# A decoder block on one core: pair tiles for the up projection, three batches of down sums, and partial sums written back into PSUM

## The chip, the core and the metric

The kernel runs on one core of a Trainium2 chip. The core has a matrix engine (TensorE, PE in the profile; PEld is its weight load), a vector engine (VectorE, DVE), a scalar engine (ScalarE, ACT), GpSimd (POOL) and SyncE (SP), which here only issues transfers. PE writes to PSUM, eight banks of 128 x 512 float32; the other engines read and write PSUM and the on-chip memory SBUF. Transfers from the chip's memory (DMA) are issued by SP, by ScalarE or by POOL. The metric is the device time of one execution in microseconds, as the median of several runs. The profile is one execution, taken by the hardware profiler.

## What is computed

One decoder block over 256 tokens with 2048 features, in float32:

```python
mod = silu(c) @ w_ada + b_ada                       # 2048 -> 6 x 2048
sh1, sc1, g1, sh2, sc2, g2 = split(mod, 6)
h = rms_norm(x, norm1_g) * (1 + sc1) + sh1
q, k, v, gb, gc, xt = split(h @ w_in, 6)            # w_in: 2048 x 6144, six parts of 1024
attn = causal attention of 8 heads of 128, q and k normalised per head
conv = gb * causal_dwconv(gc * xt, conv_w, conv_b)  # 3 taps along the tokens
mixed = concat(rms_norm(attn), rms_norm(conv))
x = x + g1 * (mixed @ w_out)                        # w_out: 2048 x 2048
h2 = rms_norm(x, norm2_g) * (1 + sc2) + sh2
u = causal_dwconv(h2 @ w_ffn_up, ffn_conv_w, ffn_conv_b)   # 2048 x 11264, 3 taps
u_gate, u_up = split(u, 2)
out = x + g2 * ((silu(u_gate) * u_up) @ w_ffn_down) # 5632 x 2048
```

The sequence has one block of 256 tokens, so the block-sparse attention of the full model is plain causal attention here.

## The kernel before

**Matmuls in two parts.** Every weight tile (128 x 2048 float32, 1 MB, "raw") is split into a rounded part `hi` (ScalarE, L329, `split_hi`) and a remainder `lo` (VectorE, `split_lo`, which shows as L166, the line of a wrapper through which most VectorE instructions are issued). Activations are split likewise. A product is hi x hi, hi x lo and lo x hi, all accumulated in PSUM.

**Slots.** The work is a list of slots, one weight tile each. A slot has its load, its size and a function that issues its matmuls. The last loop of the kernel goes through the slots; weights are split two slots ahead (`la`). Everything else is a task put at a slot with `at(slot, function)`: eviction, attention steps, convolutions, norms. Inside a slot tasks are sorted by a class from the table `cls`; the lists `x_first` and `hi_late` say for each slot whether splits come before or behind its tasks and matmuls. Each engine then runs its instructions in the order in which they were issued. Transfers of weights are issued by SP in the order in which the slots need them, together with the ada tiles (w_ada, 96 tiles of 1 MB), six or seven tiles ahead.

**Ada.** An `Ada` object makes some columns of `mod`: `consume` takes one tile and multiplies it with silu(c), either on PE (L396) or by VectorE's multiply-adds (L387, L389); `evac` and `cols` bring the sums into columns by transposes (L453). The list `ada` says at which slots. The first two (`ada_init`, scale and shift of the first 256 features) are consumed before slot 0; the next ones at slots 0 to 2. `gate_rows` places the 16 tiles of the last gate, and `fill` puts some ada tiles next to the second norm.

**Start.** x is loaded and transposed (`xn_tr`), normalised from PSUM by VectorE (`xn_norm`), shift and scale are made, and slot 0 runs in `go_first` (L583) with its own splitting in two halves.

**In projection: slots 0 to 47.** `turns` lists which of the twelve column groups of 512 (q0, q1, k0, ...) are advanced by which part of the 16 blocks of 128 input features. A pair (q0 and q1) takes two blocks a slot, a single group four. Each group has two banks (128 tokens each). Uses of a group at most three slots apart (`near`) stay in PSUM; otherwise `evac_in` empties the banks at the end: by a ScalarE copy into `pacc` the first time (L531), by a VectorE addition after that.

**Attention, short convolution, out projection.** Heads and convolution run as tasks during the rest of the in projection and the out projection (16 slots). The second norm follows at `N_OUT`.

**Up projection.** One unit is a group of 256 gate and 256 up columns: four slots of 16 + 16 matmuls in four banks (L1057 with both token parts, 512 wide, and L1060, 256 wide; the first groups use L1042). `up_sum` empties the banks into `ub`: ScalarE copies one half (L838), VectorE adds the other. `up_conv` and `up_conv_b` convolve gate and up columns (L806, L817 on ScalarE, additions on VectorE), `up_silu` and `up_gate` follow.

**Down projection.** The groups 0 to 15 are multiplied in half-slots (`A`: three products, 9 matmuls; `B`: four, 12 matmuls; L994 to L998), which form sums of a seven-product scheme. They lie between the up slots as `places` says. The groups come in batches; within a batch each of the four sets (column half, A or B) is summed over its groups in PSUM, then evicted by ScalarE (`evac_sum`, L934) and sent by POOL to memory, where later batches are added (L938, L940). `join_load` and `join_sum` fetch and combine them. The last six groups are multiplied plainly at the end (slots `LAST0` on), and `evac_down` writes the output.

## Time and profile before

| | us |
|---|---|
| median of 3 runs | 1146.89 (1146.16 to 1148.3) |
| profiled execution | 1144.87 |
| its span, first to last instruction | 1143.1 |
| PE busy in the span | 1128.9 (6035 matmuls and as many weight loads) |
| VectorE busy | 1064.0 |
| ScalarE busy | 730.6 |
| POOL busy | 61.3 |
| moved by DMA | 363.66 MB, 318 GB/s in the mean |

Busy times are the union of an engine's instructions in the profile. Matmuls overlap, so PE can be busy without going at its best pace; the pace is read from how much time a row of equal matmuls takes. A row of the groups gives line, engine, operation, output and inputs, shapes and count, then busy time and the mean of one in ns, then the engine's idle time just before and what ended it. A row of the timeline gives start and length in us. In the chain of work that ended last, each piece follows the one that released it.

### The profile page before, as it was taken

How to read it: one execution, taken by the hardware profiler on the slowest of the kernel's cores; microseconds unless marked ns; L12 is line 12 of the kernel's file. 1: busy time of each engine (PE TensorE's matmuls, PEld its weight loads, DVE VectorE, ACT ScalarE, POOL GpSimd, SP SyncE). 2: the span in 40 equal slices, each digit the busy share in tenths (PEclk: the TensorE clock that was granted, in tenths of full speed). 3: DMA queues.
4: the chain of work that ended last, by engine and by line, in shares of the span. 5: the costliest groups of instructions: out<-in, count | busy, mean ns of one | idle time of the engine just before them, and what ended most of it. 6: DMA issues, size and time to landing. Idle time of an engine off the chain costs nothing.

```text
span 1143.1 us, 16244 instructions
## 1 busy us (share of the span) xinstructions
PE 1128.9 (99%) x6035; PEld 953.8 (83%) x6035; DVE 1064.0 (93%) x1163; ACT 730.6 (64%) x1090; POOL 61.3 (5%) x90
## 2 busy tenths in 40 slices
PE   6999999999999999999999999999999999999998
PEld 4777778888888889988888888888888888888887
DVE  4789989989999998889999999899999999999798
ACT  4644455576786555566687676777677768866731
POOL 1000000000000000000000000101011101111000
PEclk9999999999999999999999999999999999999999
DMA  9999998998898899987679887999899988999951
GB/s 362 407 413 399 412 370 300 415 381 306 331 395 315 288 317 356 330 278 243 215 244 370 308 292 245 315 361 297 312 275 339 318 315 265 350 318 298 366 224 74
DMA packets 198687, 363.66 MB, mean 318 GB/s; under 512 B 9408, under 2 KB 108180, under 8 KB 194000
## 3 DMA queue, kind: packets, MB, share of 16 engines
q1 hardware_dynamic: 189152, 343.44, 82.8%
q0 software_dynamic: 8160, 17.04, 6.8%
q10 hardware_dynamic: 1296, 2.16, 0.5%
q8 instruction: 47, 0.77, 0.2%
q14 instruction: 32, 0.26, 0.1%
HBM read 343.70 MB, written 18.89 MB: 317 GB/s over the span
## 4 chain that ended last, share of the span: by engine, by line
PE 93%; DVE 3%; DMA 2%; SPq 1%; ACT 1%; issue 0%; DVEq 0%; ACTq 0%
PE z L1057 25%; PE z L1060 13%; PE u L996 4%; PE u L998 4%; PE u L994 4%; PE z L1042 4%; DMA raw<-in_w_in_dram 2%; DVE lo L166 2%; PE mk L516 1%; PE mk L517 1%; PE mk L514 1%; PE mx L516 1%; PE mc L516 1%; PE mq L517 1%; PE mg L516 1%; PE mx L517 1%
## 5 line engine op out<-in xcount | busy, mean ns | idle before, releaser
L329 ACT ACTIVATE hi<-raw 128x2048 fp32r<-128x2048 f32 (+1 forms) x227 | 417.8, 1857 | 260.5 <-DMA raw<-in_w_in_dram 73.2
L166 DVE TENSOR_TENSOR lo<-raw,hi 128x2048 fp32r<-128x2048 f32 (+2 forms) x229 | 501.7, 2200 | 23.0 <-ACT hi L329 17.7
L1057 PE MATMUL z<-h,hi 128*128 128x512 f32 x1280 | 303.3, 390 | 0.2 <-DVE ub L166 0.2
L1057 PEld LDWEIGHTS z<-h,hi 128*128 128x128 f32 x1280 | 237.8, 188 | 49.5 <-ACT hi L329 0.8
L389 DVE SCALAR_TENSOR_TENSOR ada<-raw,csil,ada 128x512 f32<-128x512 f32 (+3 forms) x167 | 195.7, 1175 | 5.3 <-DMA raw<-in_w_ada_dram 1.8
L1060 PEld LDWEIGHTS z<-h,lo 128*128 128x128 f32 x1280 | 163.1, 191 | 5.6
L1060 PE MATMUL z<-h,lo 128*128 128x256 f32 x1280 | 165.0, 283 | 0.0
L996 PE MATMUL u<-hi,gh 128*128 128x512 f32 x224 | 88.1, 393 | 0.0
L998 PE MATMUL u<-hi,gl 128*128 128x512 f32 x224 | 87.7, 392 | 0.0
L994 PE MATMUL u<-lo,gh 128*128 128x512 f32 x224 | 61.4, 390 | 0.0
L806 ACT ACTIVATE uy<-ub,fc,fc 128x256 f32<-128x256 f32 x88 | 47.6, 596 | 12.8 <-DVE ub L166 12.7
L938 POOL DMA_DIRECT2D down_sums<-pu x42 | 36.6, 1287 | 304.1 <-ACT pu L934 304.1
L996 PEld LDWEIGHTS u<-hi,gh 128*128 128x128 f32 x224 | 42.2, 188 | 9.9 <-ACT pu L934 2.8
L994 PEld LDWEIGHTS u<-lo,gh 128*128 128x128 f32 x224 | 42.0, 188 | 9.1 <-DVE lo L166 0.3
L998 PEld LDWEIGHTS u<-hi,gl 128*128 128x128 f32 x224 | 42.2, 189 | 7.4
L817 ACT ACTIVATE tap<-ub,fc 128x256 f32<-128x256 f32 x96 | 41.7, 502 | 0.0
L166 DVE TENSOR_TENSOR ub<-z,ub 128x256 f32<-128x256 f32 x96 | 33.8, 413 | 6.8 <-ACT ub L838 6.8
L301 DVE TENSOR_TENSOR raw<-raw 128x1024 f32<-128x1024 f32 x32 | 39.0, 1218 | 0.9 <-DMA raw<-in_w_ffn_down_dram 0.9
L1042 PE MATMUL z<-h,hi 128*128 128x256 f32 x256 | 36.4, 284 | 0.2 <-ACT h L765 0.2
L838 ACT ACTIVATE ub<-z 128x256 f32<-128x256 f32 x96 | 28.6, 383 | 12.1 <-PE z L1057 12.1
L166 DVE TENSOR_TENSOR uy<-tap,uy 128x510 f32<-128x510 f32 (+1 forms) x48 | 32.8, 684 | 2.0 <-ACT tap L817 0.2
L166 DVE SCALAR_TENSOR_TENSOR uy<-ub,fc,uy 128x254 f32<-128x254 f32 (+1 forms) x80 | 33.6, 477 | 0.6
(460 smaller groups left out, 1764.7 us busy)
## 6 DMA issues: line engine op xcount, KB each, us to landing
raw<-in_w_ada_dram SPq DMA_DIRECT2D x96, 1024.0 KB, 7.5
raw<-in_w_ffn_up_dram SPq DMA_DIRECT2D x176, 512.0 KB, 6.1
raw<-in_w_in_dram SPq DMA_DIRECT2D x47, 1024.0 KB, 8.0
raw<-in_w_ffn_down_dram SPq DMA_DIRECT2D x44, 1024.0 KB, 9.3
raw<-in_w_out_dram SPq DMA_DIRECT2D x16, 1024.0 KB, 6.0
raw<-in_w_ffn_down_dram SPq DMA_DIRECT2D x32, 512.0 KB, 5.0
down_sums<-pu POOLq DMA_DIRECT2D x56, 256.0 KB, 8.3
raw<-in_w_ffn_down_dram SPq DMA_DIRECT2D x32, 256.0 KB, 5.4
```

The source lines that it names most:

```text
L166: f(*a, **k)
L329: act(hi[:, :n], t[:, :n], AF.Copy)
L389: W.scalar_tensor_tensor(out=self.acc, in0=t[:, j, :], scalar=csil[:, i:i + 1], in1=self.acc, op0=ALU.mult, op1=ALU.add)
L516: mm(o, a, hi[:, k, s], start=(first and k == 0), stop=False)
L806: act(y[:, s], b[:, s], AF.Identity, bias=bias[:, i + j:i + j + 1], scale=w[2][:, i + j:i + j + 1])
L817: act(z[:, s], b[:, s], AF.Copy, scale=w[2 - d][:, i + j:i + j + 1])
L994: mm(bank_of(key), a, lo[:, n], start=False, stop=j in ends)
L996: mm(bank_of(key), a, hi[:, n], start=key not in begun, stop=False)
L998: mm(bank_of(key), b, hi[:, n], start=False, stop=False)
L1042: mm(o, w[:, j, a], h2T[k + j][:, v * 256:v * 256 + 256], start=begins and j == 0 and w is hi and not v, stop=ends and j == 3 and v == 1)
L1057: mm(zp[grp][ft], hi[:, j, ft * P:(ft + 1) * P], h2T[k + j], start=begins and j == 0, stop=ends and j == 3 and not late)
L1060: mm(zp[grp][ft][:, :256], lo[:, j, ft * P:(ft + 1) * P], h2T[k + j][:, :256], start=False, stop=ends and j == 3 and late)
```

## The change

Parts of it, with the names of the code:

- **Start.** Small matmuls that compute nothing needed (`keep_busy`, 34 in all) are put between the first steps. The last shift tile is loaded as two halves and multiplied in two steps; two one-column matmuls with a selecting vector replace its transposes and reduction. Slot 0's weights come in four DMAs instead of two, and its split, h and remainder are divided otherwise between ScalarE and VectorE. `norm_at` moves seven of the eight normalisations: four behind the first h products, three behind slot 0's split.
- **Seeds.** Where a group is taken up again, ScalarE copies `pacc` back into its two banks one slot before (`seed_in`), the matmuls accumulate onto that, and ScalarE copies the result out. Groups begun at the slots in `unseeded` keep the VectorE addition. Transposes set their start flag once a bank (`tr128`).
- **Pair tiles.** An up unit is now 512 gate columns (even units) or 512 up columns (odd units) of two groups, loaded by one DMA. Convolution, silu and product of both groups follow the units. ScalarE takes a second tap for the gate half.
- **Three batches.** Groups 0 to 5, 6 to 10 and 11 to 15 instead of four times four.
- **Columns.** Five small tables are transposed into one bank and evicted at once (`ffn_cols`).
- **Order.** `turns` exchanges neighbours (k before the second c, the first single g before x, c before v1); `places`, `gate_rows`, `fill_at`, the lists of lags and classes, `join`, `spill`, `back`, `x_first` and `hi_late` have new values.

```diff
-  [[0, 1, 2, 3], [4, 5, 6, 7], [8, 9, 10, 11], [12, 13, 14, 15]], [[0, 'A'], [1, 'A'], [0, 'B'], [1, 'B']],
-  [[0, 0, 3, 3], [0, 0, 0, 2, 2, 3], [1, 3], [1, 3, 3], [3], [0, 0, 0, 1, 1, 2, 2, 2, 3, 3], [1, 3],
-   [2, 2, 3], [3], [0, 0, 1, 1, 1, 2, 2, 2, 2, 3, 3], [1], [1, 3], [0, 0, 1, 1, 2, 2, 3, 3, 3],
-   [0, 0, 2, 3, 3], [2, 2, 2, 3, 3, 3], [0, 0, 2, 3, 3]]
+  [[0, 1, 2, 3, 4, 5], [6, 7, 8, 9, 10], [11, 12, 13, 14, 15]], [[0, 'A'], [1, 'A'], [0, 'B'], [1, 'B']],
+  [[], [0, 1], [0, 0, 0, 1, 2, 2, 2, 2, 2, 3], [0, 1, 3], [1, 1, 3], [1, 2, 3], [0, 1, 2, 3],
+   [0, 1, 2, 2, 3, 3, 3], [0, 1], [0, 0, 1, 3, 3], [0, 2, 3, 3], [0, 2, 2, 2, 3], [1, 2, 2, 3, 3, 3], [1, 3],
+   [0, 1, 2, 3, 3], [0, 2, 3]]
-  'join': [[-5, 1], [-2, 6]],       'fill_at': [0, 14, 11],   'taps': [1, 1, 2, 6],
+  'join': [[-6, 0], [0, 4]],        'fill_at': [-2, 16, 10],  'taps': [1, 2, 2, 6],
-  'spill': [6, 9],  'back': [-2, 0, -1, 1],  'up': [[0, 2, 2, 4], [0, 0, 0, 0]],
+  'spill': [9, 12], 'back': [-7, 2, -3, 5],  'up': [[0, 1, 2, 6], [0, 2, 1, 4], [0, 1, 1, 3], [0, 0, 0, 0]],
+  'busy': [9, 4, 5, 5, 5, 6],  'seed_lead': 1,  'norm_at': [1, 5, 8],
+  'unseeded': [0, 1, 2, 3, 4, 5, 6, 7, 8, 9, 10, 11, 12, 14, 15, 18, 19, 23, 39, 40, 41],
...
         if first:
-            mainp[key] = [bank(f"m{key}{t}") for t in range(3 if halves else 2)]
+            on_seed[key] = key in seeded
+            if key in seeded:
+                seeded.remove(key)
+                first = False
+            else:
+                mainp[key] = [bank(f"m{key}{t}") for t in range(3 if halves else 2)]
...
                 act(pacc[f, t], p, AF.Copy)
+            elif now[0] - 1 in unseeded.get(f, ()):
+                V.tensor_tensor(out=pacc[f, t], in0=p, in1=pacc[f, t], op=ALU.add)
             else:
-                V.tensor_tensor(out=pacc[f, t], in0=p, in1=pacc[f, t], op=ALU.add)
+                act(pacc[f, t], p, AF.Copy)
+    def seed_in(f):
+        mainp[f] = [bank(f"m{f}{t}") for t in range(2)]
+        for t in range(2):
+            act(mainp[f][t], pacc[f, t], AF.Copy)
+        seeded.add(f)
...
+            if i != uses[f][0] and not near(f, -1):
+                begun[f] = i
+                if i not in CFG["unseeded"]:
+                    at(len(slots) - 1 - CFG["seed_lead"], seed_in, f)
...
-            slots.append((w_load(w_up, k, 4, [(grp * 256, 256), (DFF + grp * 256, 256)]), 4, go))
+            slots.append((w_load(w_up, k, 4, [(grp % 2 * DFF + grp // 2 * 512, 512)]), 4, go))
...
+            w = grp % 2
+            for n, (f, *a) in zip(lag, ((up_conv, 0, w), (up_conv, 1, w), (up_gate if w else up_silu, 0), (up_gate if w else up_silu, 1))):
+                at(UP_SLOTS[-1] + 1 + hold + n, f, grp - w + a[0], *a[1:])
...
+    def keep_busy(b, n):
+        for _ in range(n):
+            mm(b[:, 256:384], onesr, onesr, start=True, stop=True)
...
+    keep_busy(p_one, w2)
+    sh.products(0, 0, 8)
     xn_tr(6, 7)
+    keep_busy(p_one, w3)
+    xn_norm(*range(5, n1))
+    sh.products(1, 0, 4)
+    sh.products(1, 4, 8)
+    keep_busy(p_one, w4)
+    rows_sum = t2k("adae")[:, :256]
+    act(rows_sum, sh.acc, AF.Copy)
+    for k in range(2):
+        mm(p_one[:, k:k + 1], rows_sum[:, k * P:(k + 1) * P], sel, start=k == 0, stop=k == 1)
+    keep_busy(bank("two"), w5)
+    z = small(8, "adaz")[:, :2]
+    V.tensor_copy(z, p_one[:, :2])
...
+    rest(0)
+    V.tensor_copy(hi[:, 1], w[:, 1])
+    rest(1)
+    act(hi[:, 2], w[:, 2], AF.Copy)
+    V.tensor_copy(hi[:, 3], w[:, 3])
+    xn_norm(*range(n1, n2))
+    for j in range(0, 4, 2):
+        V.tensor_tensor(out=lo[:, j:j + 2], in0=w[:, j:j + 2], in1=hi[:, j:j + 2].bitcast(F32), op=ALU.subtract)
```

More of the change, by code (lines that the diff above doesn't have):

```diff
@@ L226, in tile_block, with tr128 @@
     V.tensor_copy(identb, ident)
+    ssq = const.tile([P, 32], F32, name="ssq")
+    sel = ssq[:, :1]
+    V.tensor_reduce(out=sel, in_=ident.rearrange("p (j r) -> p j r", j=4)[:, :, 0], axis=AX.X, op=ALU.add)
     rows(vb, [(by_p(norm1_g[0]), 16)], nc.gpsimd)
+    def tr128(o, v, first):
+        nc.tensor.matmul(o, lhsT=v, rhs=ident, start=first, stop=True, is_transpose=True, skip_group_check=True)
     def to_cols(v, n, name):
@@ L362, in issue, with products @@
             def issue(t):
-                nc.sync.dma_start(self.view(t), w_ada[0, k0 * P:(k0 + self.rows) * P, a:a + self.n]
-                                  .rearrange("(k p) f -> p k f", p=P))
-            return issue
+                for i, j in self.cuts.get(r, [(0, self.rows)]):
+                    nc.sync.dma_start(self.view(t)[:, i:j], w_ada[0, (k0 + i) * P:(k0 + j) * P, a:a + self.n]
+                                      .rearrange("(k p) f -> p k f", p=P))
+            return issue
+        def products(self, r, i, j):
+            if i == 0:
+                self.used += 1
+                self.held = self.view(take((self, r)))
+            if self.acc is None:
+                self.acc = bank(f"ada{self.part}_{self.c0}")[:, :self.n]
+            for k in range(i, j):
+                q = 32 * (k % 4)
+                mm(self.acc[q:q + 32, :], crep[:, self.rows * r + k, :], self.held[:, k, :],
+                   start=r == 0 and k < 4, stop=r == self.tiles - 1 and k >= self.rows - 4,
+                   tile_position=(0, q))
+            if j == self.rows:
+                load_next()
         def home(self):
@@ L923, in gate_down @@
         done.add(f"gd{f}")
+        if f in CFG["sum_late"]:
+            return
         for t in range(2):
@@ L1498, in tile_block @@
     ada_init[0].consume(0)
+    def keep_busy(b, n):
+        for _ in range(n):
+            mm(b[:, 256:384], onesr, onesr, start=True, stop=True)
+    p_one = bank("one")
+    w0, w1, w2, w3, w4, w5 = CFG["busy"]
+    keep_busy(p_one, w0)
     pr = bank("n1b")
@@ L1511, in xn_norm @@
                             in1=rT.unsqueeze(1).to_broadcast([P, 2, 256]), op=ALU.mult)
-    xn_norm(0, 1, 2, 3)
-    ada_init[0].consume(1)
-    ada_init[0].evac()
-    ada_init[0].cols()
-    xn_norm(4)
+    sc, sh = ada_init
+    n0, n1, n2 = CFG["norm_at"]
+    xn_norm(*range(n0))
+    sc.consume(1)
+    keep_busy(p_one, w1)
+    sc.evac()
+    sc.cols()
+    hf = []
+    b1 = SH1 * NK
+    for k in range(2):
+        hf.append(t1k("hf"))
+        V.tensor_scalar(hf[k], xnT[0][:, k * 256:(k + 1) * 256], A1[:, k:k + 1], bcol[:, b1 + k:b1 + k + 1],
+                        op0=ALU.mult, op1=ALU.add)
@@ L1527, in tile_block @@
+    keep_busy(bank("two"), w5)
+    z = small(8, "adaz")[:, :2]
+    V.tensor_copy(z, p_one[:, :2])
     w = take(("w", 0))
     hi, lo = (sb.tile([P, 4, 512], F32R, tag=g, bufs=N_HL, name=g) for g in ("hi", "lo"))
-    parts = [(slice(2 * k, 2 * k + 2), t1k("hf"), t2k(f"h{k}", F32R)) for k in range(2)]
-    b1 = SH1 * NK
-    for k, (s, h, hk) in enumerate(parts):
-        hT[k] = halves(hk)
-        V.tensor_scalar(h, xnT[0][:, k * 256:(k + 1) * 256], A1[:, k:k + 1], bcol[:, b1 + k:b1 + k + 1],
-                        op0=ALU.mult, op1=ALU.add)
@@ L1548, in tile_block, with rest @@
-    for s, _, _ in parts:
-        V.tensor_tensor(out=lo[:, s], in0=w[:, s], in1=hi[:, s].bitcast(F32), op=ALU.subtract)
+    done.update((SH1, k) for k in range(2))
+    hk = [t2k(f"h{k}", F32R) for k in range(2)]
+    act(hi[:, 0], w[:, 0], AF.Copy)
+    for k in range(2):
+        hT[k] = halves(hk[k])
+        if k:
+            act(hT[k][0], hf[k], AF.Identity, bias=z[:, k:k + 1])
+        else:
+            V.tensor_scalar(hT[k][0], hf[k], z[:, k:k + 1], None, op0=ALU.add)
+    def rest(k):
+        V.scalar_tensor_tensor(out=hT[k][1], in0=hf[k], scalar=z[:, k:k + 1], in1=hT[k][0].bitcast(F32),
+                               op0=ALU.add, op1=ALU.subtract)
```

210 lines of the change are left out of this document (107 added, 103 removed), and 12 rows, old and new, of the table CFG.

## The prediction

> **What bounds the kernel now.** I read the page's busy times first, then busy time by stretch, PE's waits, and the chain of work that ended last in order of time.
>
> ```profile
> span 1143.1 us, 16244 instructions
> PE 1128.9 (99%) x6035; PEld 953.8 (83%) x6035; DVE 1064.0 (93%) x1163; ACT 730.6 (64%) x1090; POOL 61.3 (5%) x90
> ```
>
> ```profile
> core 0: us, PE busy (x) PEld busy (x) DVE busy (x) ACT busy (x) POOL busy (x), PEclk, DMA share, GB/s
> 0.00:22.00 22.00, 12.74 (x106) 8.48 (x106) 9.47 (x27) 9.79 (x15) 5.24 (x16) 1.00 0.95 348
> 22.00:26.00 4.00, 3.58 (x9) 2.86 (x10) 1.37 (x3) 1.82 (x3) 0.00 (x0) 0.57 1.02 420
> 26.00:42.00 16.00, 15.93 (x85) 12.13 (x87) 13.61 (x16) 9.65 (x11) 0.00 (x0) 1.00 1.07 397
> 170.00:320.00 150.00, 150.00 (x726) 123.85 (x725) 142.68 (x142) 97.86 (x219) 2.56 (x2) 1.00 0.91 344
> 870.00:970.00 100.00, 100.00 (x531) 86.09 (x530) 98.36 (x99) 73.13 (x94) 9.60 (x11) 1.00 0.95 305
> ```
>
> ```profile
> PE ada L396 <- DMA raw<-in_w_ada_dram: 1.2, 3, 0.5
> PE mx L516 <- ACT pa_g L531: 0.5, 1, 0.5
> PE z L1042 <- ACT h L765: 0.2, 1, 0.2
> PE z L1057 <- DVE ub L166: 0.2, 1, 0.2
> PE mq L517 <- DVE hl L166: 0.2, 1, 0.2
> ```
>
> ```profile
> 15.16 13.36 DMA raw<-in_w_in_dram
> ...
> 37.12 12.37 DMA raw<-in_w_in_dram
> ...
> 492.16 7.28 PE z L1057 x32
> 499.44 3.83 PE z L1060 x32
> ```
>
> The reader is to see four things. PE is busy 99% of the span, and the idle part lies before 22 us (12.74 of 22.00 busy); in the two later stretches shown it is never idle. A busy PE might still hide waits, so I look at its pace: the chain gives 7.28 us for 32 matmuls of 512 columns, 0.2275 us each, and 3.83/32 = 0.12 us for 256 columns. That pace holds through the chain, so PE runs at its issue rate. All waits of PE after 22.5 us that the list shows come to under 2 us. And up to about 50 us the chain runs over the weight DMAs (13.36 us, then 12.37 us), with a DMA share above 1 in the rows from 22 to 42 us. So a change can win at the start only if data lands sooner, later only those few waits; VectorE, at 93%, is a close second that nobody yet waits for.
>
> Here the row meets a rule that speaks for a gain. The Trainium skill ("Perfetto Trace Analysis", Identifying the Most-Contended Engine) says that matmul busy time misleads because matmuls overlap, and that the weight loads' busy share should be read instead. Here that is 83%, which by the rule would leave up to 17% to win. The constant 0.2275 us speaks against room of that kind.
>
> **The change, part by part.** The sum is made against the profiled execution, 1144.87 us: 1143.1 of span and 1.8 around it. The median of the runs shown, 1146.89, is 2.0 above; I add it at the end. Inside 0.2% (2.3 us) a run of this kernel can't be told from no change.
>
> *The start.* Rows of the first 42 us:
>
> ```profile
> 17.60 2.58 DVE L166 TENSOR_TENSOR xnT<-xn,n1rT 128x512 f32<-128x512 f32 x4
> 19.61 1.07 PE L396 MATMUL ada<-raw,crep 128*32 128x256 f32 x16 [0.54 <-DMA raw<-in_w_ada_dram]
> 20.74 0.38 ACT L417 ACTIVATE adae<-ada 128x256 f32<-128x256 f32 x1 [5.01 <-PE ada L396]
> 20.89 0.69 DVE L166 CAST hi<-raw 128x1024 fp32r<-128x1024 f32 x1
> 21.18 0.44 PE L453 MATMUL adac<-ident,adae 128*128 128x128 f32 x2 [0.50 <-ACT adae L417]
> 21.66 0.17 DVE L166 TENSOR_REDUCE adaz<-adac 128x2 f32<-128x8 f32 x1
> 21.86 0.51 ACT L1542 ACTIVATE h<-hf,adaz 128x256 fp32r<-128x256 f32 x1 [0.73 <-DVE adaz L166]
> 22.42 5.43 PE L583 MATMUL mc<-hi,h 128*128 128x512 f32 x16 [0.80 <-ACT h L1542]
> 23.62 1.06 ACT L1544 ACTIVATE hi<-raw 128x1024 fp32r<-128x1024 f32 x1 [1.26 <-DMA raw<-in_w_in_dram]
> 25.51 2.35 DVE L166 TENSOR_TENSOR lo<-raw,hi 128x1024 fp32r<-128x1024 f32 x2
> 29.50 0.39 PE L516 MATMUL mv<-hi,h 128*128 128x512 f32 x1
> 41.87 0.59 PEld L396 LDWEIGHTS ada<-raw,crep 128*32 128x32 f32 x16 [0.49 <-DMA raw<-in_w_ada_dram]
> ```
>
> The last shift tile now lands in two halves: only 8 of its 16 products are left when the second lands, so they end near 19.61 + 0.54 = 20.15. The ScalarE copy (0.38), two one-column matmuls for the two transposes (at most 0.44), one VectorE copy for the reduction (0.17) and the first h on VectorE (at most 0.51) follow: the first matmul near 21.5, 0.9 us sooner. The keep-busy matmuls, 34 of 128 columns at no more than 0.12 us each, go into idle PE time before that. But the second half of the weights lands at 23.62 as before. On VectorE the second cast (0.69/2) ends at 23.97; three normalisations are moved in behind it (3 x 2.58/4 = 1.94), so the two low parts (2.35) end at 28.26, and four matmuls later (0.9) the slot ends at 29.2 instead of 29.5: 0.3 us sooner.
>
> That lead meets the row at 41.87. There PE waits 0.49 us for an ada tile, executed in order behind slot 2. The change leaves the order of the loads up to there as it is, and the queue is full, so that tile lands at the same time, and a PE that comes earlier waits longer. I take 0 for the start; bounds: -2.7 (the 0.9, and 5.43 - 16 x 0.2275 = 1.8 of slow matmuls, if the tile lands sooner) and +0.5 (lead lost, low parts late). Single-bank column loads and one eviction for five are off the path: 0.
>
> *Seeding.* By the turns list, the code sums 54 tiles on VectorE now and 24 after; 14 weight groups (28 tiles) are instead written by ScalarE into PSUM one slot early, and copied out by ScalarE.
>
> ```profile
> L166 DVE TENSOR_TENSOR pa_g<-mg,pa_g 128x512 f32<-128x512 f32 x12 | 7.6, 681 | 0.0
> 30.43 2.04 ACT L531 ACTIVATE pa_c<-mc 128x512 f32<-128x512 f32 x4
> L881 ACT ACTIVATE gh<-uy 128x512 fp32r<-128x512 f32 x22 | 13.6, 633 | 6.5 <-DVE uy L166 6.5
> ```
>
> VectorE loses 30 x 0.68 = 20 us. ScalarE gains 28 copies out at 2.04/4 = 0.51, and 28 writes that the trace doesn't show: between 0.51 (reading PSUM) and 0.63 (SBUF to SBUF), I take 0.57 as the path lies between the two; 30 us together. They fall between slots 16 and 47, about 110 to 320 us, where ScalarE is busy 97.86 of 150 (170 to 320); two thirds of them there make it about 118 of 150. Cover: the split of weights runs two slots ahead, and a slot is 24 x 0.2275 = 5.5 us. A ScalarE command queued behind a seed (the next split, an attention step) is 1.1 us later. The seed waits for two free banks; the next slot's first matmul then waits for the seed, written a whole slot earlier. 0; bounds -0.2 and +1.5 (one late split at each of three crowded slots, 0.5 each).
>
> *Pair tiles, three batches.*
>
> ```profile
> raw<-in_w_ffn_up_dram SPq DMA_DIRECT2D x176, 512.0 KB, 6.1
> L934 ACT ACTIVATE pu<-u 128x512 f32<-128x512 f32 x56 | 28.7, 588 | 3.3 <-PE u L994 3.3
> L817 ACT ACTIVATE tap<-ub,fc 128x256 f32<-128x256 f32 x96 | 41.7, 502 | 0.0
> L166 DVE SCALAR_TENSOR_TENSOR uy<-ub,fc,uy 128x254 f32<-128x254 f32 (+1 forms) x80 | 33.6, 477 | 0.6
> L166 DVE TENSOR_TENSOR uy<-tap,uy 128x510 f32<-128x510 f32 (+1 forms) x48 | 32.8, 684 | 2.0 <-ACT tap L817 0.2
> 783.70 1.41 DVE L166 TENSOR_TENSOR ub<-z,ub 128x256 f32<-128x256 f32 x4
> ```
>
> The up weights come in 88 DMAs of 1 MB instead of 176 of 512 KB, the same bytes: SP issues less, PE never waited for them, 0. The matmuls stay the same in number and shape. Fourteen partial sums fewer go out: 14 x 0.588 = 8.2 us of ScalarE, 14 POOL transfers, all beside PE: 0. The first tap on ScalarE for 16 groups takes 2 x 0.477 - 0.684 = 0.27 us each off VectorE (4.3 us) and puts 2 x 0.502 each on ScalarE (16 us). ScalarE: 731 + 30 - 8 + 16 = 769 us, 67%; VectorE: 1064 - 20 - 4 = 1040, 91%.
>
> The half-slots move. Before, every unit of up matmuls but one ends with a down half-slot, under which its four banks are emptied. The one without it is at 783.70: ub's additions begin as the next unit is due, and PE waits 0.2 us, some 0.5 with its restart. After, two units end so with a batch open: +0.5. The wait at z L1042 (0.2) stays. Where VectorE was just in time, 24 us less work could spare me about as much: -0.5. Bounds of this part: -1.0 and +4.8 (below).
>
> *What only moves.* Two of the four fill products go ahead of the second norm instead of into it: the same PE work in the same gap, so the wait at z L1042 can move by its 0.2 either way. The 16 loads of the last gate change slots, each with a VectorE sum, in SP's queue between weight loads that are there over a slot ahead; the spill of x1 (ScalarE's queue) goes later, its return (SP's) up to five slots earlier or four later, ahead of its use. Other order lists say only whether a split goes before or after the work of its slot. I take 0, covered by the lead of the splits; without that cover, one split late costs its slot at most 0.5, which is in the bounds of the parts above.
>
> *The tail.* The last matmul, addition and store don't change. Sums for the down outputs are joined earlier or later by slots of 5.5 us, before the slots that need them. 0, bounds -0.2 and +0.5.
>
> Sum: 0 + 0 + 0.5 - 0.5 + 0 = 0. So 1144.9 against the profiled execution, 1146.9 in terms of the median.
>
> **The rivals.** *The start pays (faster).* The granted clock is 0.57 from 22 to 26 us, which is 0.43 x 4 / 0.5 = 3.4 us at half speed, and the first 16 matmuls took 5.43 us. If the keep-busy matmuls hold the clock, the chain to z is shorter and the tile at 41.87 lands sooner too, all 2.7 us come through: 1144.2. For it: the clock. Against: the DMA chain of 13.36 and 12.37 us, whose order is kept. Chance 0.14. The Trainium skill ("TensorE: Matmul & The Clock Gate", Part 1: The HAM clock gate) says that the clock halves after an idle window of about 3.4 us and returns after a busy one, which agrees with the 3.4 us worked out above; by it the 1.8 us would be won, if nothing behind them waits.
>
> *PE hides waits (faster).* If the weight loads' 83% is the true load, 24 us less on VectorE could show whole: 1123. The constant pace leaves 0.03.
>
> *Bursts of pairs (slower).* Gate and up columns of two groups now end together: convolutions, two products and two roundings fall behind one unit, 2.7 us of tap additions (4 x 0.684) and 1.4 of products in a row, where VectorE is at 98.36 of 100. The lows of the next half-slots queue behind. If the burst outlasts the lead by 0.3 to 0.6 us at each of eight pairs, PE loses 2.4 to 4.8: 1149.3 to 1151.7, 1150.5 in the middle. It decides from 0.3 us a pair. For it: 98.36. Against: 4.3 us less work there, and a lead of up to two slots. Chance 0.20.
>
> *The change doesn't do as it says.* Only 14 of 26 later groups are seeded, the rest stay on VectorE. As nobody waits for these additions the time is the same, 1146.9; it is part of the forecast.
>
> **How the numbers follow.** Forecast (no change that can be told) 0.60; start pays 0.14, hidden waits 0.03, and 0.03 for PE's other waits all going with a little of the start (1144.5): faster 0.20. Slower 0.20. Predicted is the likeliest, 1146.9. The range reaches from just under the start's 1144.2 to the middle of the slow case: 1144.0 to 1150.5, leaving out 0.03 below and about half of the 0.20 above. The forecast's own range is 1145.0 to 1149.0.
>
> **What would show it.** PE's first matmul into mc near 21.5 and clock 1.00 there, but the ada product at slot 2 still near 41.9 behind a longer DMA wait: the start as told. If it comes at 40 or earlier, the start's rival holds. VectorE near 1040 us and ScalarE near 770: the exchange as counted. Seeds of 0.51 to 0.63 us, none followed by a wait of PE. Waits of PE for ub at two units without a half-slot, 0.5 each; many waits for lo or ub between 570 and 1070 would make the prediction wrong upward, PE starting slots of the in projection over 1 us sooner after 60 us wrong downward.

## The result: 8.6 us slower, and the profile after

The changed kernel takes 1155.04 us in the median (1153.51 to 1157.06), the kernel before, run beside it, 1146.47 (1144.93 to 1148.3). The ratio is 1.0078, 95% interval 1.0066 to 1.0089. That is outside the predicted range (1144.0 to 1150.5). The profiled execution took 1153.51 us; its page begins:

```profile
span 1151.7 us, 16091 instructions
PE 1132.5 (98%) x6072; PEld 956.8 (83%) x6072; DVE 1046.5 (91%) x1120; ACT 762.2 (66%) x1160; POOL 49.4 (4%) x76
```

VectorE lost 17.5 us of work and ScalarE gained 31.6, close to what was counted (1040 and 769 us were forecast). PE did the same work but for 37 small matmuls more, 34 of them the keep-busy ones, and yet the span is 8.6 us longer. The head of the list of PE's waits after 22.5 us (total us, times, longest):

```profile
PE m('D', 3)2_10285 L550 <- DVE d L172: 1.4, 1, 1.4
PE n2b L791 <- DVE n2d L172: 1.2, 1, 1.2
PE z L1110 <- DVE ub L172: 1.0, 1, 1.0
PE m('D', 0)0_9944 L548 <- DVE lo L172: 0.9, 1, 0.9
PE mc L630 <- DVE lo L172: 0.6, 1, 0.6
PE ada L424 <- DMA raw<-in_w_ada_dram: 0.4, 1, 0.4
```

Five of these six name VectorE, the engine that was relieved. To see where the time went, I take the start of the same slot in both traces, with PE's work in between set equal where half-slots moved. PE is behind by 1.5 us at the first up matmul, 3.4 at the first matmul of the last stage, 6.8 after the last matmul, and 8.6 at the end of the span. The rows for the first three, of the timeline of PE, before and then after:

```profile
425.92 0.74 PE L1042 MATMUL z<-h,hi 128*128 128x256 f32 x4 [0.24 <-ACT h L765]
1073.74 0.40 PE L516 MATMUL m('D', 0)0_10003<-hi,gh 128*128 128x512 f32 x1
1139.11 0.64 PE L514 MATMUL m('D', 3)2_10339<-lo,gh 128*128 128x256 f32 x4
```

```profile
427.40 0.74 PE L1095 MATMUL z<-h,hi 128*128 128x256 f32 x4 [0.24 <-ACT h L818]
1077.18 0.50 PE L550 MATMUL m('D', 0)0_9944<-hi,gh 128*128 128x512 f32 x1
1145.86 0.64 PE L548 MATMUL m('D', 3)2_10285<-lo,gh 128*128 128x256 f32 x4
```

So there are three places: 1.5 us up to the second norm, 1.9 in the up stage, and 3.3 + 1.9 in the last stage (up to the last matmul, and behind it).

**The last stage.** The timeline of VectorE before and then after, where it first needs the last gate (`ju<-ju,ada`, `gate_down`):

```profile
1089.73 4.48 DVE L166 TENSOR_TENSOR lo<-raw,hi 128x2048 fp32r<-128x2048 f32 x2
1094.13 0.68 DVE L166 TENSOR_TENSOR ju<-ju,ada 128x512 f32<-128x512 f32 x1
```

```profile
1089.50 6.78 DVE L172 TENSOR_TENSOR lo<-raw,hi 128x2048 fp32r<-128x2048 f32 x3
1102.46 0.69 DVE L172 TENSOR_TENSOR ju<-ju,ada 128x512 f32<-128x512 f32 x1 [6.18 <-DMA ada<-gate_sums]
```

VectorE stands still for 6.18 us, until the broadcast of the gate lands. Before, it had no such wait, and it had no room for one either: it was busy 9.93 of 10 us from 1090 to 1100.

```profile
1090.00:1100.00 10.00, 10.00 (x46) 8.28 (x45) 9.93 (x9) 4.01 (x5) 0.00 (x0) 1.00 1.05 407
```

(PE, weight loads, VectorE, ScalarE, POOL, clock, DMA share, GB/s; 10 us of before.) After the gap VectorE works without a pause to 1147.9; PE waits for its low parts and for a bank (0.9 and 1.4 us above), and the end of the additions after the last matmul comes another 1.9 us later. Why the gate is late stands on POOL's queue, before and then after:

```profile
1052.63 3.49 POOL L938 DMA_DIRECT2D down_sums<-pu  x4 [29.72 <-ACT pu L934]
1069.08 1.97 POOL L433 DMA_DIRECT2D gate_sums<-adar  x4 [12.97 <-ACT adar L431]
1076.36 0.56 POOL L439 DMA_DIRECT2D ada<-gate_sums  x1 [5.31 <-DMA gate_sums<-adar]
```

```profile
1080.56 3.49 POOL L991 DMA_DIRECT2D down_sums<-pu  x4 [41.15 <-ACT pu L987]
1082.72 3.28 POOL L461 DMA_DIRECT2D gate_sums<-adar  x4
1094.58 0.56 POOL L467 DMA_DIRECT2D ada<-gate_sums  x1 [8.58 <-DVE lo L172]
```

The last four partial sums, which are added in memory, left 16 us ahead of the gate's four small writes; now they leave straight ahead of them. The writes land 10.2 us after their issue instead of 5.1 (median of the four), straight behind the last of the partial sums (1093.3, then 1093.5 to 1094.0), and the broadcast goes out only then. (The row names a VectorE release; but in every profile where no partial sums are issued between the writes and the broadcast, it goes out 0.6 to 0.7 us after the last write landed, here at 1093.96.) The Trainium skill ("DMA: Bandwidth & Descriptors", SWDGE vs HWDGE vs iDMA) says that only one queue is allocated to transfers issued by GpSimd; the doubled time behind 1 MB of accumulating transfers agrees with that.

**The second norm.** In front of the sums for the norm VectorE now adds the last scale tile, moved from slot 55 to 58. Before, then after:

```profile
418.19 0.15 DVE L166 TENSOR_REDUCE ss<-ss 128x2 f32<-128x6 f32 x1
```

```profile
416.61 3.11 DVE L417 SCALAR_TENSOR_TENSOR ada<-raw,csil,ada 128x512 f32<-128x512 f32 x4
419.63 0.15 DVE L172 TENSOR_REDUCE ss<-ss 128x2 f32<-128x6 f32 x1
```

That explains a part of the 1.5 us. 0.9 of it arises behind the fourth column block of the out projection, with the wait for `n2d`, and does so again in other profiles with the same order. The rest was there before and is not fixed: three profiles whose kernels are the same up to this point (changed kernel, gate back, half-slots early) come to that block 0.6 and 1.2 us behind the kernel before, and 0.5 ahead of it.

**The up stage.** PE loses 1.1 us at 656 (0.95 of it a wait), behind a run of half-slots. Rows of VectorE, ScalarE and PE, then 20 us of the windows (after, then before):

```profile
652.01 1.23 DVE L313 TENSOR_TENSOR raw<-raw 128x1024 f32<-128x1024 f32 x1 [2.10 <-DMA raw<-in_w_ffn_down_dram]
654.86 1.92 ACT L341 ACTIVATE hi<-raw 128x2048 fp32r<-128x2048 f32 x1 [4.25 <-DVE raw L319]
657.56 0.73 PE L1110 MATMUL z<-h,hi 128*128 128x512 f32 x2 [0.95 <-DVE ub L172]
```

```profile
640.00:650.00 10.00, 10.00 (x46) 8.28 (x45) 8.50 (x5) 6.99 (x5) 0.00 (x0) 1.00 1.04 404
650.00:660.00 10.00, 9.04 (x48) 7.48 (x47) 7.73 (x10) 5.75 (x11) 0.00 (x0) 1.00 1.04 405
```

```profile
640.00:650.00 10.00, 10.00 (x53) 8.56 (x52) 9.83 (x10) 5.07 (x4) 0.00 (x0) 1.00 0.79 265
650.00:660.00 10.00, 10.00 (x53) 8.60 (x52) 9.93 (x11) 7.96 (x14) 2.07 (x4) 1.00 1.02 368
```

The weights land late with the DMA engines full (share 1.04, 404 GB/s, where before had 0.79); VectorE's weight sums wait for them, ScalarE's next split for VectorE, the copies into `ub` queue behind that split, and PE waits for `ub`.

### The profile page after: what moved, and what is told of

Read it like the earlier page. It is cut to its first block, busy times and chain, and to the rows that moved or that the text cites. A ratio compares the mean times of both kernels' runs of the same rounds, so it can differ in the third digit from the quotient of the medians.

```text
span 1151.7 us, 16091 instructions
## 1 busy us (share of the span) xinstructions
PE 1132.5 (98%) x6072; PEld 956.8 (83%) x6072; DVE 1046.5 (91%) x1120; ACT 762.2 (66%) x1160; POOL 49.4 (4%) x76
## 4 chain that ended last, share of the span: by engine, by line
PE 85%; DVE 7%; DMA 5%; issue 1%; ACT 1%; SPq 0%; DVEq 0%; ACTq 0%
PE z L1110 23%; PE z L1113 12%; PE z L1095 4%; PE u L1047 4%; PE u L1051 4%; PE u L1049 4%; DVE lo L172 3%; DMA raw<-in_w_in_dram 2%; DMA raw<-in_w_ffn_down_dram 2%; PE mk L550 1%; PE mk L551 1%; PE mk L548 1%; PE mx L550 1%; PE mc L550 1%; PE mq L551 1%; PE mg L550 1%
## 5 line engine op out<-in xcount | busy, mean ns | idle before, releaser
L1110 PEld LDWEIGHTS z<-h,hi 128*128 128x128 f32 x1280 | 238.2, 188 | 50.4 <-DVE ub L172 1.9
L870 ACT ACTIVATE tap<-ub,fc 128x256 f32<-128x256 f32 x128 | 54.5, 506 | 0.0
L859 ACT ACTIVATE uy<-ub,fc 128x256 f32<-128x256 f32 x88 | 48.0, 601 | 8.8 <-DVE ub L172 8.6
L172 DVE TENSOR_TENSOR uy<-tap,uy 128x510 f32<-128x510 f32 x64 | 43.9, 685 | 3.5 <-ACT tap L870 0.2
L991 POOL DMA_DIRECT2D down_sums<-pu x28 | 24.4, 1287 | 283.4 <-ACT pu L987 283.4
L1095 PEld LDWEIGHTS z<-h,hi 128*128 128x128 f32 x256 | 33.2, 192 | 0.5 <-ACT h L818 0.5
```

The lines of the kernel that those rows point to most:

```text
L172: f(*a, **k)
L859: act(y[:, s], b[:, s], AF.Identity, bias=bias[:, i + j:i + j + 1], scale=w[2][:, i + j:i + j + 1])
L870: act(z[:, s], b[:, s], AF.Copy, scale=w[2 - d][:, i + j:i + j + 1])
L1095: mm(o, w[:, j, a], h2T[k + j][:, v * 256:v * 256 + 256], start=begins and j == 0 and w is hi and not v, stop=ends and j == 3 and v == 1)
L1110: mm(zp[grp][ft], hi[:, j, ft * P:(ft + 1) * P], h2T[k + j], start=begins and j == 0, stop=ends and j == 3 and not late)
```

## The experiments

One table first, since the same three places are read in every trace: PE's lag behind the kernel before at the first up matmul, its growth from there to the last stage, and its growth within the last stage up to the last matmul. These come from one profile each; the column "that run" is the time of that execution, which can lie some us off the median. "Of it clock" is the part of the two growths in which the granted clock was below 1.00 (time at half clock, halved).

| kernel | at first up matmul | + up stage | + last stage | of it clock | that run | median us | ratio to before |
|---|---|---|---|---|---|---|---|
| changed kernel | 1.5 | 1.9 | 3.3 | 0 | 1153.51 | 1155.04 | 1.0078 |
| gate back | 0.4 | 3.2 | 0.0 | 0 | 1148.93 | 1151.17 | 1.0043 |
| before, gate late | -0.2 | 1.2 | 0.1 | 0 | 1145.96 | 1145.79 | 0.9998 |
| no seeds | 1.5 | 7.6 | 3.8 | 3.4 | 1159.69 | 1156.16 | 1.0092 |
| no keep-busy | 0.7 | 3.2 | 4.8 | 0 | 1155.43 | 1153.18 | 1.0068 |
| scale tile back | 2.8 | 5.7 | 0.0 | 0 | 1153.87 | 1153.56 | 1.0059 |
| half-slots spread | 2.7 | 4.2 | 0.0 | 0 | 1152.00 | 1153.65 | 1.0060 |
| half-slots early | 2.1 | 10.6 | 0.1 | 3.4 | 1157.86 | 1157.24 | 1.0089 |
| before, half-slots and gate late | -0.3 | 2.0 | 9.6 | 1.7 | 1156.12 | 1156.11 | 1.0083 |
| loads back | 0.2 | 12.5 | 4.0 | 1.7 | 1163.51 | 1164.20 | 1.0150 |
| loads and gate back | 0.1 | 12.4 | 0.0 | 1.7 | 1157.56 | 1159.19 | 1.0114 |
| loads in light units | 0.0 | 13.9 | 0.0 | 3.4 | 1159.01 | 1159.96 | 1.0121 |
| pairs, four batches | 0.1 | 14.5 | 0.7 | 3.4 | 1160.39 | 1161.84 | 1.0135 |
| the same, old order | 1.6 | 15.2 | 0.7 | 3.4 | 1162.51 | 1162.03 | 1.0137 |
| before, three batches | 2.0 | 9.9 | 5.3 | 3.4 | 1164.23 | 1162.98 | 1.0143 |
| gate's sums first | 1.0 | 3.5 | 0.1 | 0 | 1150.01 | 1149.88 | 1.0038 |
| memset moved | 1.4 | 7.9 | 0.0 | 3.4 | 1154.61 | 1152.84 | 1.0051 |

So a wait of PE can cost more than itself. In the trace of "no seeds" PE waits 3.19 us, and the 12 matmuls behind the wait take 5.49 us, 0.46 each instead of 0.2275; the granted clock (third figure from the end of the second row) is 0.50 there:

```profile
659.85 5.49 PE L1110 MATMUL z<-h,hi 128*128 128x512 f32 x12 [3.19 <-DVE ub L172]
660.00:665.00 5.00, 5.00 (x12) 3.94 (x13) 4.97 (x7) 5.00 (x12) 0.99 (x2) 0.50 0.99 351
```

Each such stretch lasts about 3.4 or 6.8 us and so costs 1.7 or 3.4. It does not follow every wait: one of 2.7 us at the same place in "no keep-busy" left the clock at 1.00. The changed kernel's own trace has none.

### The gate back

```diff
-'slag': [[2, 2], [0, 3]],
+'slag': [[2, 2], [-1, 2]],
```

> The changed kernel with one pair of numbers set back: the sums of the last gate are taken one slot before the tail and spread at slot 2 of it (slag of G2 -1, 2 instead of 0, 3). Theory (the gate's broadcast holds VectorE 6.2 us in the tail, and VectorE has no idle time after that): the wait for gate_sums goes, PE reaches its last matmul about 3.3 us sooner and the end after the last matmul shrinks from 5.2 to 3.3 us; about 5 us less than the changed kernel, 1150 us. Rival (the tail is long because its sums and evictions were reordered, joins at 0 and 4, evac_down in the last class): at most 1 us less, 1154 us.

Measured 1151.17 (1148.93 to 1151.76), 3.9 us less than the changed kernel; the wait for the gate is gone, and the last stage adds nothing up to the last matmul (0.6 us stays behind it). The theory held for the place; some 4 of the 5 us that it forecast came off.

### The gate late in the kernel before

```diff
-'slag': [[1, 2], [-1, 2]],
+'slag': [[1, 2], [0, 3]],
```

> The kernel before with only the last gate's sums and spread put later (slag of G2 0, 3 instead of -1, 2). Theory (gate broadcast alone makes the tail long): VectorE waits about 5 us for gate_sums around slot 3 of the tail and the time rises by 3 to 5 us over before, 1150 to 1152 us. Rival (it takes the other moves of the change as well): within 1 us of before.

Measured 1145.79 (1144.41 to 1148.77), ratio 0.9998 (0.9988 to 1.0007). My theory fell: the broadcast lands at 1092.6, still ahead of VectorE, which is due at the gate at 1094.6. So the later slot by itself costs nothing, and "the gate is late" is not yet the cause.

### No seeds

```diff
+'unseeded': list(range(48)),
```

> The changed kernel without any seed: all later sums of the in projection are VectorE additions again, all else as changed. Theory (seeds are off PE's path): the time stays within 1 us of the changed kernel, 1154 to 1156 us; VectorE 20 us busier and ScalarE 30 us less busy. Rival (the seeds cost part of the 8.6 us, by bank waits or a crowded ScalarE): 2 us or more less than the changed kernel.

Measured 1156.16 (1153.76 to 1159.69), though VectorE was busy 1062.2 us again and ScalarE 736.5. Seeding neither wins nor loses anything that can be told.

### No keep-busy matmuls

```diff
-'busy': [9, 4, 5, 5, 5, 6],
+'busy': [0, 0, 0, 0, 0, 0],
```

> The changed kernel without the 34 keep-busy matmuls. Theory (PE waits at about 42 us for an ada tile whose landing is fixed by the transfers): the granted clock falls to half for about 3.4 us near slot 0 again, slot 0 takes up to 1.5 us longer, but slot 4 starts within 0.5 us of the changed kernel (50.0 us) and the total stays within 1 us of it. Rival (keep-busy matmuls win time that is kept): 1.5 us or more slower than the changed kernel; or, if they delay the first steps, about 0.5 us faster.

```profile
22.00:26.00 4.00, 4.00 (x11) 3.13 (x12) 3.67 (x8) 0.78 (x2) 0.00 (x0) 0.60 1.03 421
```

The clock in the first slot is 0.60 in this profile and 1.00 in the changed kernel's. That the small matmuls make the difference is not shown: of the four profiles of kernels with the old start, which has none of them, the kernel before shows 0.57, but the three others (gate late, half-slots and gate late, three batches) show 1.00. The row of "gate late":

```profile
22.00:26.00 4.00, 3.57 (x14) 2.46 (x15) 1.99 (x3) 2.38 (x4) 0.00 (x0) 1.00 1.02 418
```

There slot 0 ends at 28.37 us instead of 29.50 before, and of these 1.1 us 0.2 are left at the first up matmul. So the clock at the start wins little that lasts, and the time without the small matmuls is not longer: 1153.18 (1152.82 to 1155.43), ratio 1.0068 (1.0053 to 1.0083), an interval that overlaps the changed kernel's. PE's first matmul into mc comes at 21.96 us without them, against 22.3 to 23.2 in nearly all profiles with them, so they may hold up the first steps by some 0.5 us.

### The scale tile back, with the gate back

```diff
-[3, 8, 512, False, 58, 7]
+[3, 8, 512, False, 55, 7]
```

> The changed kernel with the last gate's sums and broadcast again one slot before the last stage (as in the run that put them back alone, 1151.2), and with the tile of the second norm's scale, columns 8 to 15, loaded from slot 55 again instead of 58. Theory: the 3.1 us of that tile's VectorE additions at 416.6 stand ahead of the second norm's sums and delay the first up matmul by about 1.4 us, so this one ends at 1149.9 (1149.4 to 1150.3), PE's wait n2b <- n2d of 1.2 us is gone, and the first up matmul starts within 0.5 us of where it starts before. Rival: the lag at the norm comes from the attention and the output projection ahead of it (other classes), and the additions are hidden: 1151.2, the wait stays.

Measured 1153.56 (1151.38 to 1154.37), 2.4 above the run with the gate back: a miss. The additions no longer stand ahead of the norm, but in the out projection, where VectorE has almost no gap either (9.76 of 10 us from 380 to 390), and PE waits 1.5 us for a low part up to 389. At the norm the wait stayed, for another reason:

```profile
424.91 1.80 POOL L399 MEMSET ada<- 128x2048 f32 x1 [91.11 <-DVE n2r L172]
424.94 1.92 DVE L172 TENSOR_SCALAR n2d<-ident,n2r 128x128 f32<-128x128 f32 x2
```

Two scalings that take 0.48 us in the kernel before took 1.92 beside GpSimd's filling of the gate's sum tile. The changed kernel loads that gate from up slot 4 on instead of 11, which brings the filling to the norm.

### Half-slots spread

```diff
-[[], [0, 1], [0, 0, 0, 1, 2, 2, 2, 2, 2, 3], ... [0, 1],
+[[1, 3], [0, 1, 3], [0, 1, 1, 2, 2, 2, 3], ... [0, 3],
```

> The run with the scale tile at slot 55, and four half-slots of the down projection moved within the list: two into the first unit, one into the second, so that the run of six in the third unit's place 2 is shorter, and one moved in the ninth unit so that it ends with a half-slot. Theory: the stall of 1.1 to 1.6 us at 656 us comes from a unit that ends without a half-slot after a run of them, during which the splits of the weights are late; spread out, both units' stalls (1.1 to 1.6 at 656, 0.2 at 748) go and this one ends 1.3 to 1.8 us under the run with the scale tile alone, about 1148.3. Rival: the stall follows from the pairs themselves (additions into ub late behind the partner's convolution) and stays or moves to another unit: no difference.

This is on top of the run before. Measured 1153.65 (1152.0 to 1153.88), no difference from it: the stall came one unit earlier (the lag grows from 2.8 to 4.4 us between 620 and 640). The rival, "moves to another unit", held.

### Half-slots early, gate late

```diff
-[0, 1, 2, 3, 3], [0, 2, 3]]
+[0, 1, 2, 3, 3], [0, 0, 0]]
```

> The changed kernel with its late gate kept as it is (sums at the first slot of the last stage, broadcast at its fourth), but the last three half-slots of the down projection put right after the first up slot of the last unit instead of after its first, third and fourth, so that the last four partial sums leave ScalarE some 8 us sooner. Theory: the late gate costs only because those four copies (2.0 us) stand ahead of the gate's copy on ScalarE and their four accumulating transfers ahead of the gate's on GpSimd's queue, whose small writes then take 10 us to land instead of 5 to 6; with them gone VectorE's wait of 6.2 us falls under 1 us and the time to 1150.5 to 1152. Rival: it is the later slot by itself, in a kernel whose last stage starts 3.4 us late, and the time stays within 1 us of 1155.

The mechanism held, the time missed: the small writes land after 4.5 us, VectorE's wait is gone and the last stage adds 0.1. But the up stage adds 10.6 (three half-slots in a row bring two waits for low parts at 1058 and 1064, 3.7 us in sum; the stall at 659 is 2.5; half clock costs 3.4), and the time is 1157.24 (1155.5 to 1157.86).

### Half-slots and gate late in the kernel before

```diff
-[0, 0, 2, 3, 3], [2, 2, 2, 3, 3, 3], [0, 0, 2, 3, 3]]   'join': [[-5, 1], [-2, 6]],   'slag': [[1, 2], [-1, 2]],
+[0, 0, 2, 3, 3], [2], [0, 2, 3]]                       'join': [[-5, 1], [0, 6]],    'slag': [[1, 2], [0, 3]],
```

> The kernel before with the late gate (which alone made no difference) and, of the change, one more thing: the last four half-slots of the down projection at the end of the list (after slots 1, 3 and 4 of the last unit and one before), so that their partial sums leave as the last stage begins, and the loads that join them two slots later. Theory: now the gate's broadcast lands after VectorE is due at it; VectorE waits 3 to 6 us near 1094 and the kernel takes 1149 to 1152. Rival: the kernel before has slack for it, 1146 to 1147.

Measured 1156.11 (1153.7 to 1157.76), ratio 1.0083: more than forecast. On POOL and on VectorE it is the pattern of the changed kernel:

```profile
1078.77 3.49 POOL L938 DMA_DIRECT2D down_sums<-pu  x4 [55.17 <-ACT pu L934]
1081.76 2.46 POOL L433 DMA_DIRECT2D gate_sums<-adar  x4
1094.89 0.56 POOL L439 DMA_DIRECT2D ada<-gate_sums  x1 [10.68 <-DVE ju L166]
```

```profile
DVE ju L166 <- DMA ada<-gate_sums: 6.3, 1, 6.3
```

The late gate that cost nothing alone now holds VectorE for 6.3 us, once the last partial sums stand ahead of it. Of the 9.6 us of the last stage 6.5 are waits of PE and 1.7 half clock. (The run also joins the second half's sums two slots later, whose share is not separated.)

### The gate's loads back; with the gate back; in light units

```diff
-'gate_rows': [3, 10, 18, 22, 30, 32, 33, 45, 49, 53, 54, 57, 59, 68, 72, 75],
+'gate_rows': [10, 14, 17, 18, 30, 35, 40, 43, 46, 51, 54, 57, 58, 64, 68, 74],   # loads back; loads and gate back
+'gate_rows': [10, 14, 18, 22, 24, 26, 28, 30, 38, 40, 42, 44, 46, 48, 58, 66],   # in light units, gate back
```

> The changed kernel with one list put back: the slots at which the 16 tiles (1 MB each) of the last gate are loaded are those of the kernel before. Theory: the stalls of PE near 656 us (1.1 us in the changed kernel's trace, 1.6 to 4.4 in the traces of its variants) and near 860 us (0.4 to 3) come from three gate tiles loaded in the 30 us before a run of ten half-slots, and four in the 60 us before a run of seven; the DMA engines are full there and the weights land late. With the loads apart, PE's lag behind the kernel before grows by less than 0.5 us between 620 and 690, and the time falls by 1 to 3 us, to 1152 to 1154. The tail's wait for the gate stays. Rival: the runs of half-slots alone fill the DMA engines and VectorE; the stall stays above 1 us and the time within 1 us of 1155.

> The changed kernel with the last gate's loads at the slots of the kernel before, and its sums and broadcast at theirs (which alone gave 1151.2). Theory: the two causes add; the tail costs nothing, the stalls of the up stage are gone, and what stays is the 1.3 us at the second norm and the end: 1148 to 1149.5. Rival: the stall at the runs of half-slots stays: 1151 to 1152.

> As the run with both put back, but the last gate's 16 loads stand at slots of units that hold few half-slots or none (five of them from the first two units on, none beside the runs of seven and ten). Theory: the loads collide with the half-slots' weights, so this is no slower than the run before, 1147.5 to 1149, and the share of the DMA engines from 600 to 640 us is lower. Rival: the loads only move the crowding into the units where VectorE is busy already, and a wait of 1 us or more appears there: 1150 to 1152.

My theory fell: 1164.2 (1159.17 to 1164.92), 1159.19 (1155.84 to 1160.42) and 1159.96 (1159.01 to 1160.39). In the first of them PE waits at three units' ends (655, 720 and 753 us) instead of one, and at two of these VectorE has an addition of the last gate straight ahead of the additions into `ub` (at 655.38, shown, and at 719.73):

```profile
PE z L1110 <- DVE ub L172: 6.0, 3, 2.8
655.38 2.35 DVE L417 SCALAR_TENSOR_TENSOR ada<-raw,csil,ada 128x2048 f32<-128x2048 f32 x1
657.64 1.41 DVE L172 TENSOR_TENSOR ub<-z,ub 128x256 f32<-128x256 f32 x4
```

Each of the 16 loads brings VectorE 2.35 us and the DMA engines 1 MB, and both other lists that I tried were worse than the changed kernel's. So taking the loads away from the runs of half-slots does not lift the stalls; at two of these three waits it is the 2.35 us on VectorE that stand in the way. The gate back took 5.0 us off here as well (1164.2 to 1159.19).

### Pairs with four batches, also with the old order; three batches without pairs

The first has the changed code with the old `plan`, `gate_rows`, `join`, `slag`, `gate`, `back`, `spill` and the old classes of `join_sum` and `evac_down`; the second also the other old classes (but for `up_conv_b`), `x_first`, `hi_late`, `ada`, `qk`, `evac`, `sq` and `tr`; the third is the kernel before with the change's values of the first list.

> The changed kernel's code with pair tiles and seeding, but with the four batches of the kernel before, its places of the half-slots, its slots for the last gate's loads, sums and broadcast, and its steps of the tail (joins, gate, spill, and the order of the last sums and evictions). Theory (the placement costs, not the pairs): the tail's 3 to 5 us are gone as in the run with the gate put back, the stalls at the units' ends stay under 1 us in sum, and what is left is the 1 to 1.5 us at the second norm: 1147 to 1149. Rival (pairs cost: convolutions and products of two groups come in one burst, and the units' ends without a half-slot wait for VectorE's additions): waits of 3 us and more for ub or lo between 570 and 1070 us: 1150 to 1156.

> As the run with four batches, and nearly all other order numbers of the kernel before as well (which of a slot's tasks goes first, the splits' order lists, the scale tile at slot 55); of the change there stay the start, the seeding and the pair tiles with their own steps. Theory: the second norm's 1 to 1.5 us go too, 1145.5 to 1147, no difference from before that can be told. Rival (pairs cost): 1149 to 1155; the tasks' order was part of what made pairs possible, and it may be slower than the run with four batches.

> The kernel before, without pairs, seeding or the new start, with three batches and the changed kernel's places of half-slots, its slots for the last gate's loads, sums and broadcast, and its steps of the tail. Theory (the placement costs): VectorE waits 3 to 6 us for the gate near 1096 us, PE loses 3 to 5 us in the tail and 1 to 5 us at the runs of half-slots: 1150 to 1156. Rival (it is the pairs): 1146 to 1148.

All three are slower than the changed kernel, and than all that I had forecast for them: 1161.84 (1160.39 to 1162.56), 1162.03 (1161.12 to 1164.39) and 1162.98 (1162.09 to 1164.23). The first, pairs with the old places, has its largest wait (half clock follows it) where the old list puts half-slots behind the first slot of the first unit:

```profile
PE u L1049 <- DVE ub L172: 4.8, 1, 4.8
```

That place is empty in the change. The third, without pairs, seeds or the new start, has stalls at the changed kernel's unit ends (1.6 us at 658) and a wait for the gate of 8.2 us. So neither the pairs alone nor the placement alone is faster. That pairs need the half-slots later, and that these then bring the runs and the late partial sums, is my reading; each list was fitted to its own kernel, and no run separates that. These runs do part the 0.9 us at the second norm. With the gate's loads at their old slots, and so no memset at the norm, 0.5 is left (the first run, and the three runs with other load slots); with the scale tile back at 55 as well (the second, which comes to that block 1.6 us late) nothing is left.

### The gate's sums first

```diff
-'sum_rows': 1,
+'sum_rows': -2,
```

> The changed kernel with its late gate kept at its slots; of the first slot of the last stage's tasks, the gate's sums go first instead of last, so that on ScalarE the gate's copy stands ahead of the last four partial sums (2.0 us) and on GpSimd's queue the four small writes ahead of the four accumulating transfers of 256 KB. Theory: the small writes land after about 5 us instead of 10, the broadcast goes out 5 to 7 us sooner, VectorE's wait of 6.2 us near 1096 falls under 2 us, and the time to 1151 to 1153. Rival: the wait follows from the late slot, whatever stands ahead; it stays above 4 us and the time within 1 us of 1155.

```profile
1081.60 1.97 POOL L461 DMA_DIRECT2D gate_sums<-adar  x4 [41.26 <-ACT adar L459]
1083.57 3.56 POOL L991 DMA_DIRECT2D down_sums<-pu  x4
1088.05 0.56 POOL L467 DMA_DIRECT2D ada<-gate_sums  x1 [0.92 <-PE m('D', 1)1_9985 L551]
```

Measured 1149.88 (1148.96 to 1155.75), ratio 1.0038 (1.0023 to 1.0053): 5.2 us less than the changed kernel by the medians, 4.6 by the ratios, and a little more than forecast. (The class holds for both gates, so the first gate's sums, near 323 us, move within their slot as well; the lag at the first up matmul, 1.0 us, is within what the other profiles show.) The gate's writes start 1.1 us sooner, land after 4.3 us instead of 10.2, the broadcast goes out 6.5 us sooner, and VectorE has no wait for it. This isolates the cause in the last stage: not the slot but what stands ahead of the gate's sums in it. Of the 6.5 us, 1.1 come from the earlier start of the last of the four writes and 5.4 from its shorter landing.

### The memset moved

```diff
-'gate_rows': [3, 10, 18, ...     (with the scale tile and the gate back)
+'gate_rows': [6, 10, 18, ...
```

> As the run with the scale tile at slot 55 (1153.6), with the first of the last gate's loads at the seventh up slot instead of the fourth, and with it the filling of its sum tile by GpSimd (1.8 us), which in that run began 0.03 us before VectorE scaled the identity for the second norm: those two scalings then ended after 1.92 us instead of 0.48. Theory: VectorE waits for GpSimd there; the scalings take 0.48 us again, PE's wait for them (1.2 us) and its lag at the first up matmul (2.8 us) shrink by 1.2 to 1.4, and the time by 1 to 1.5 if nothing later absorbs it. Rival: the scalings are slow because of their place behind the out projection's evictions; they stay at 1.9 us.

```profile
424.87 0.48 DVE L172 TENSOR_SCALAR n2d<-ident,n2r 128x128 f32<-128x128 f32 x2
```

The scalings take 0.48 us again, PE's wait for them is gone and the lag at the first up matmul is 1.4 instead of 2.8 us: the theory held there. In time little came through, 1152.84 (1150.09 to 1154.61) against 1153.56: in this profile the up stage adds 7.9 instead of 5.7, and half clock is 3.4 of it.

No version of the changed kernel came down to the kernel before; the nearest was the one with the gate's sums first.

## Why the prediction was wrong, step by step

- **What bounds the kernel.** PE at its issue rate held in both. "VectorE ... a close second that nobody yet waits for" was true and not enough: in the last stage (9.93 of 10 us) VectorE had no gap, and in the out projection almost none (9.5 to 10.0 of every 10 us from 325 to 415), so a wait or an addition that is put there can come out at PE. I read shares over the span and two stretches, neither of them the last 70 us. The rival of hidden waits fell: the weight loads' share is 83% again, and 17.5 us less work on VectorE made nothing faster.
- **The tail: the step that failed.** It was taken as 0, with +0.5 as its bound, because "sums for the down outputs are joined earlier or later by slots of 5.5 us, before the slots that need them". That looked at the joins only. It left out that the last gate's sums come one slot later (`slag`), that the last partial sums are sent by POOL from that same slot, ahead of the gate's on ScalarE and POOL, and that VectorE's gate products wait for the last of that chain. Size 5.2 us: 3.3 up to the last matmul and 1.9 behind it; with the order turned round 0.7 of it is left in the profile, and 4.6 to 5.2 came off the time.
- **What only moves.** Taken as 0, "covered by the lead of the splits". Of the 1.5 us lag at the first up matmul, 0.9 arises between the fourth column block of the out projection and there: 0.3 at the memset that the gate's moved loads bring to the norm, and the rest, as far as one run tells, at the additions of the moved scale tile. With the gate back, moving the tile back only moved the wait. The lead of the splits did not cover steps on which the norm itself waits. The other 0.6 differs from profile to profile.
- **Pair tiles, three batches.** +0.5 for units that end without a half-slot with -0.5 for relief; the up stage cost 1.9, with one such end, at 656, at 1.1 against the 0.5 given to it. The right place, the size too small by half or more; no relief came. The prediction's slower rival, bursts of pairs, had the sign, but its steady 0.3 to 0.6 us at each pair is not seen: 1.1 of the 1.9 come at one place, and the three batches without pairs stalled there too. A burst's part in that stall is not excluded.
- **The start.** 0, as forecast, and by its mechanism in the end, the wait for the tile; the lead of 0.9 us before it did not come. PE's first matmul into mc came at 23.15, not 21.5 (22.3 to 22.6 in the profiles of most variants with this start, 25.3 in one; 22.42 in the kernel before). The first 16 matmuls ran at clock 1.00 in 3.92 us instead of 5.43, then waited for the low part behind the moved normalisations, and then for the same ada tile:

```profile
23.15 3.92 PE L630 MATMUL mc<-hi,h 128*128 128x512 f32 x16
27.62 2.33 PE L630 MATMUL mc<-lo,h 128*128 128x512 f32 x8 [0.55 <-DVE lo L172]
42.50 0.85 PE L424 MATMUL ada<-raw,crep 128*32 128x256 f32 x12 [0.36 <-DMA raw<-in_w_ada_dram]
```

- **Seeds.** 0, as forecast. The price taken for the write into PSUM was 0.57 us; the groups give 0.58 to 0.64 by column group, like the copy out:

```profile
L576 ACT ACTIVATE mv<-pa_v 128x512 f32<-128x512 f32 x6 | 3.4, 612 | 0.0
L569 ACT ACTIVATE pa_v<-mv 128x512 f32<-128x512 f32 x6 | 3.2, 592 | 0.0
```

**What stays open.** The up stage. Its growth lies between 1.9 us in the changed kernel and 15 in its variants, and single profiles of kernels with the same up stage differ by several us (1.9, 3.2 and 7.6; in the last, half clock is 3.4). VectorE and the DMA engines are both near full there, and no run separated the two. How much of the 1.5 us before it comes again in every execution is open too.

## What to carry to other kernels

Where a step is moved, follow its last product through every queue it shares, that of the small transfers too, and ask what then stands behind it: 2 KB writes behind 1 MB of accumulating ones took twice as long and held up the busiest helper. Relieving an engine by 17.5 us, most of it in one stage, wins nothing in another stage where it has no gap; read its gaps stage by stage, up to the end. And when a schedule is fitted by hand, parts of a change put back alone can be slower than the whole, so test the suspected order directly, as moving one kind of task to the front of its slot did here. And read every row of a single profile beside other profiles of the same code: here the lag before the second norm and the clock differed between them by as much as the effects looked for.

## What the hardware showed that I had not expected

VectorE's TENSOR_SCALAR of 128x128 float32, 0.29 us each, took 1.72 and 1.85 us beside a GpSimd memset of 1.8 us that had begun 0.03 us earlier, and the trace books all of it as work. VectorE's three-operand additions beside another such memset kept their 0.75 us. The other way round, a memset of that size that began 0.15 us after a TENSOR_SCALAR of 128x1024 took 2.36 us (at 176.3 in the changed kernel). The Trainium skill ("SBUF — State Buffer", SBUF: two separate sides) says that one pair of ports is shared by the two engines under an exclusive lock, held for a whole instruction, which VectorE needs in its fast modes; the two runs, with and without the memset, agree.
